# Cutting the last row of a streamed loss kernel into six pieces instead of seven

## The chip, the cores and the metric

One core of a Trainium2 chip runs the kernel. The metric is the device time of one execution in microseconds (us). A time is the median of several runs, with lowest and highest in brackets where they matter.

In the traces the semaphore of each load got 16 updates, spread over 0.38 to 0.44 us in the old kernel's profile. Here a load counts as landed at the last of them, when its semaphore is full. Where a text counts "from the row-6 landing", it means the moment at which the last load before the changed part (row 6 of the target) has landed.

## The reference

```python
batch, dim = 1024, 4096
log_input = randn(batch, dim) as float32
target    = randint(0, 10, (batch, dim)) as float32

def reference(log_input, target):
    loss = np.exp(log_input) - target * log_input
    return np.mean(loss, axis=-1).astype(np.float32)
```

Two arrays of 16 MiB are read once, and 4 KiB are written.

## The kernel before

Each of the 128 partitions owns eight rows of 4096 columns. x is `log_input`, t is `target`. Rows 0 to 6 are loaded in large transfers; the last row (row 7) is cut into pieces, given in units of 32 columns:

```python
TAIL = [("x", 98), ("t", 50), ("t", 48), ("x", 24), ("t", 18), ("x", 6), ("t", 12)]
# ... cut ...
for what, w in TAIL:
    loads.append((what, at[what], w * d // 128))
    at[what] += w * d // 128
```

All loads go out in this order from one queue. ScalarE (ACT in the profile) takes exp of each x piece and sums it along the row; VectorE (DVE) multiplies each t piece with its x and sums -t*x. In the profile each of these is followed by a short row with READ_ACCUMULATOR in its name (0.08 us on DVE, 0.19 on ACT), whose output is one column:

```python
nc.vector.tensor_tensor_reduce(            # every product but the last
    out=place("t", lo, w), in0=place("t", lo, w), in1=place("x", lo, w),
    scale=-1.0, op0=ALU.mult, op1=ALU.add, accum_out=...   # cut
).wait_op(landed[i], 16, "sem-ge").then_inc(
    prod_done if j < n_t - 2 else last_ready, 1)
```

The partial sums of row 7 are written into spare columns right behind the last piece of t, opposite columns of x that hold -1. So one last product over the last t piece and these columns gives the finished mean, and it must wait for three things at once:

```python
nc.vector.tensor_tensor_reduce(            # the last product
    in0=place("t", lo, w + n_parts), in1=place("x", lo, w + n_parts),
    scale=-inv_d, op0=ALU.mult, op1=ALU.add,               # cut
    accum_out=all_loss[:, last_row : last_row + 1],
).wait_op(last_ready, 18, "sem-ge")        # 16: its own load; 1: last exp sum; 1: last product sum
```

Then SP, which issues all 14 transfers in the profile, stores the 4 KiB result.

## Time and profile before

| | before |
|---|---|
| time | 83.93 us (83.86 to 84.18, 3 runs) |
| span in the profile | 82.5 us |
| load queue | 2016 packets, 33.56 MB, 95.8% of 16 engines' span |
| DVE busy / ACT busy | 43% / 40% |

The span is counted from the first load to the last instruction; the time is about 1.34 us longer (83.89 for the profiled run of span 82.545). Busy shares of DVE and ACT are averages over the whole span and say little here: DVE waited 45.4 us of the span for loads and ACT 23.6, and both matter only in the last microseconds (in the 10 us windows from 40 to 80 us the DMA share was 0.98 to 1.01). The prediction below shows the lines themselves.

### The profile page before, as it was taken

The numbers are of one execution on the slowest core, as the hardware profiler recorded it, in microseconds if no ns is written. First come the engines' busy times: TensorE is split into PE (matmuls) and PEld (weight loads), VectorE is DVE, ScalarE is ACT, GpSimd is POOL, SyncE is SP. The second block draws the span as 40 slices with busy tenths as digits, with TensorE's granted clock in tenths as the row PEclk, the third lists the DMA queues.
The fourth block names the chain that finished last, engine by engine and source line by source line (L and its number), as shares of the span: only waits on it lengthen the run. The fifth ranks groups of instructions, "written<-read, shape, count | busy, mean of one in ns | idle before, by whom it ended". The sixth has DMA issues, their size and how long they took to land.

```text
span 82.5 us, 131 instructions
## 1 busy us (share of the span) xinstructions
DVE 35.6 (43%) x22; ACT 33.2 (40%) x35; POOL 0.3 (0%) x5
## 2 busy tenths in 40 slices
DVE  0000000000000000000099999999369995993992
ACT  0500000000499920000000998979792496009460
POOL 0000000000000000000000000000000000000000
DMA  9289999929999992999599799799799999999960
GB/s 508 127 381 508 508 508 508 476 95 445 508 508 508 508 413 95 508 508 508 254 508 429 333 508 492 318 460 508 302 453 397 461 421 418 426 402 412 397 231 2
DMA packets 2016, 33.56 MB, mean 407 GB/s; under 512 B 352, under 2 KB 608, under 8 KB 1120
## 3 DMA queue, kind: packets, MB, share of 16 engines
q1 hardware_dynamic: 2016, 33.56, 95.8%
HBM read 33.55 MB, written 0.00 MB: 407 GB/s over the span
## 4 chain that ended last, share of the span: by engine, by line
DMA 72%; DVE 18%; issue 5%; SPq 3%; DVEq 0%
DMA t_big<-in_target_dram 49%; DMA x_big<-in_log_input_dram 23%; DVE t_big L175 17%; SPq L129 3%; DVE t_big L193 1%; DVE parts L175 0%; DVEq L192 0%; SPq L127 0%; DVE all_loss L193 0%
## 5 line engine op out<-in xcount | busy, mean ns | idle before, releaser
L175 DVE CUSTOM_DVE_ANT_0 t_big<-t_big,x_big 128x4096 f32<-128x4096 f32 (+3 forms) x8 | 26.2, 3308 | 43.5 <-DMA t_big<-in_target_dram 43.4
L155 ACT ACTIVATE e_dump<-x_big 128x4096 f32<-128x4096 f32 (+3 forms) x8 | 21.8, 2729 | 23.9 <-DMA x_big<-in_log_input_dram 23.6
L141 ACT ACTIVATE join_dump<-parts 128x2 f32<-128x2 f32 x7 | 1.4, 203 | 20.4 <-DVE parts L175 20.3
L175 DVE CUSTOM_DVE_ANT_0 t_mid<-t_mid,x_mid 128x4096 f32<-128x4096 f32 x2 | 8.8, 4424 | 2.0 <-DMA t_mid<-in_target_dram 2.0
L155 ACT ACTIVATE e_dump<-x_mid 128x4096 f32<-128x4096 f32 x2 | 7.1, 3568 | 0.0
L155 ACT ACT_TABLE_LOAD x1 | 1.3, 1283 | 2.9 <-PEq L48 2.9
L155 ACT ACTIVATION_READ_ACCUMULATOR e_dump<-x_big 128x1 f32 x8 | 1.5, 186 | 0.0
L141 ACT ACTIVATION_READ_ACCUMULATOR join_dump<-parts 128x1 f32 x7 | 1.3, 186 | 0.0
L175 DVE DVE_READ_ACCUMULATOR2_ANT parts<- 128x1 f32 x7 | 0.6, 84 | 0.0
L193 DVE CUSTOM_DVE_ANT_0 t_big<-t_big,x_big 128x390 f32<-128x390 f32 x1 | 0.6, 566 | 0.0
L155 ACT ACTIVATION_READ_ACCUMULATOR e_dump<-x_mid 128x1 f32 x2 | 0.4, 186 | 0.0
L175 DVE DVE_READ_ACCUMULATOR2_ANT t_big<- 128x1 f32 x3 | 0.2, 82 | 0.0
L136 POOL MEMSET x_big<- 128x6 f32 x1 | 0.1, 104 | 2.5 <-POOLq L48 2.5
L227 POOL MEMSET const-uint8-127<- 128x1 uint8 x1 | 0.1, 102 | 0.0
L227 POOL MEMSET const-bfloat16-1.0<- 128x1 bf16 x1 | 0.1, 101 | 0.0
L227 POOL MEMSET const-float32-0.0<- 128x1 f32 x1 | 0.1, 98 | 0.2 <-issue 0.2
L227 POOL MEMSET const-float32-1.0<- 128x1 f32 x1 | 0.1, 98 | 0.0
L193 DVE DVE_READ_ACCUMULATOR2_ANT all_loss<- 128x1 f32 x1 | 0.1, 82 | 0.0
## 6 DMA issues: line engine op xcount, KB each, us to landing
x_mid<-in_log_input_dram SPq DMA_DIRECT2D x1, 4096.0 KB, 49.9
t_mid<-in_target_dram SPq DMA_DIRECT2D x1, 4096.0 KB, 59.2
x_big<-in_log_input_dram SPq DMA_DIRECT2D x1, 2048.0 KB, 19.8
t_big<-in_target_dram SPq DMA_DIRECT2D x1, 2048.0 KB, 24.3
x_big<-in_log_input_dram SPq DMA_DIRECT2D x1, 1568.0 KB, 15.4
t_big<-in_target_dram SPq DMA_DIRECT2D x1, 800.0 KB, 17.0
t_big<-in_target_dram SPq DMA_DIRECT2D x1, 768.0 KB, 18.4
x_big<-in_log_input_dram SPq DMA_DIRECT2D x1, 384.0 KB, 18.9
```

The costliest lines, as they stand in the source:

```text
L129: dma = nc.sync.dma_start(out=place(what, lo, w), in_=src[:, lo : lo + w])
L136: nc.gpsimd.memset(big["x"][:, 4 * d : 4 * d + n_parts], -1.0).then_inc(ones_done, 1)
L141: nc.scalar.activation(out=join_dump[:, 2 * row : 2 * row + 2], in_=parts[:, 2 * row : 2 * row + 2], func=ACT_F.Copy, scale=inv_d, accum_o ...
L155: nc.scalar.activation(out=e_dump[:, col : col + w], in_=place("x", lo, w), func=ACT_F.Exp, bias=0.0, scale=1.0, accum_out=parts[:, 2 * ro ...
L175: nc.vector.tensor_tensor_reduce(out=place("t", lo, w), in0=place("t", lo, w), in1=place("x", lo, w), scale=-1.0, scalar=0.0, op0=ALU.mult ...
L193: nc.vector.tensor_tensor_reduce(out=place("t", lo, w + n_parts), in0=place("t", lo, w + n_parts), in1=place("x", lo, w + n_parts), scale= ...
L227: nc = _bacc.Bacc("TRN2", target_bir_lowering=False, num_devices=1)
```

## The change

Merging the 192-column x piece into the x pieces before it (128 columns go to the second, 64 to the first) saves one transfer and one exp. The t pieces are made a little larger in front, and the last two equal.

```diff
-TAIL = [("x", 98), ("t", 50), ("t", 48), ("x", 24), ("t", 18), ("x", 6), ("t", 12)]
+TAIL = [("x", 100), ("t", 52), ("t", 48), ("x", 28), ("t", 14), ("t", 14)]
```

In columns: x 3136, t 1600, t 1536, x 768, t 576, x 192, t 384 become x 3200, t 1664, t 1536, x 896, t 448, t 448.

## The prediction

Its sum: +151 (landing) - 133 (second-last product) + 65 (last product) = +83 ns, which takes 83.93 to 84.01 us. Its slopes and fixed costs are fits to the old kernel's profile: 159 ns + 1.0417 ns a column to the DVE products, 175 + 0.833 to the exps, 65 ns a piece + 1.18 a column to the landings. That an engine serves 8 partitions is the division of a piece's 128 packets by the 16 engines of the profile page; it fits the trace, in which eight packets of 16384 bytes (median 611 ns each) make 4888 ns and the row-6 t landed 4891 ns after the row-6 x.

> **What bounds the kernel now.** I read the page's chain of work first, then the queue table, then the timeline of the last 9 us, then the waits, and last the trace's records of when each transfer's semaphore became full.
>
> The chain of the page says that almost three quarters of the span is transfer time:
>
> ```profile
> ## 4 chain that ended last, share of the span: by engine, by line
> DMA 72%; DVE 18%; issue 5%; SPq 3%; DVEq 0%
> ...
> q1 hardware_dynamic: 2016, 33.56, 95.8%
> ```
>
> The reader should see a single queue that keeps its 16 engines busy for 95.8% of the span while it moves 33.56 MB. All work is paced by this stream, and the change moves no byte more or less. So the only time that the cut of the last row can change is what remains between the stream's last pieces and the end. The timeline of that stretch:
>
> ```profile
> 74.10 2.79 ACT L155 ACTIVATE e_dump<-x_big 128x3136 f32<-128x3136 f32 x1 [4.44 <-DMA x_big<-in_log_input_dram]
> ...
> 76.05 1.83 DVE L175 CUSTOM_DVE_ANT_0 t_big<-t_big,x_big 128x1600 f32<-128x1600 f32 x1 [1.28 <-DMA t_big<-in_target_dram]
> ...
> 77.94 1.76 DVE L175 CUSTOM_DVE_ANT_0 t_big<-t_big,x_big 128x1536 f32<-128x1536 f32 x1
> 78.93 0.81 ACT L155 ACTIVATE e_dump<-x_big 128x768 f32<-128x768 f32 x1 [1.53 <-DMA x_big<-in_log_input_dram]
> ...
> 79.70 0.76 DVE L175 CUSTOM_DVE_ANT_0 t_big<-t_big,x_big 128x576 f32<-128x576 f32 x1
> 79.97 0.33 ACT L155 ACTIVATE e_dump<-x_big 128x192 f32<-128x192 f32 x1
> 80.24 0.19 ACT L155 ACTIVATION_READ_ACCUMULATOR e_dump<-x_big 128x1 f32 x1
> 80.38 0.08 DVE L175 DVE_READ_ACCUMULATOR2_ANT t_big<- 128x1 f32 x1
> 80.50 0.57 DVE L193 CUSTOM_DVE_ANT_0 t_big<-t_big,x_big 128x390 f32<-128x390 f32 x1
> ```
>
> The columns are start, duration, engine, line, operation. VectorE (DVE) sums -target*x for each piece of t, ScalarE (ACT) sums exp for each piece of x, and the last DVE instruction (L193) takes the last t piece together with the partial sums in the columns after it. It starts when three things are there: its own t piece, the last exp sum, and the last product sum. The landing records (semaphore full, us from the span's start) give what the timeline rounds off or leaves unnamed:
>
> ```
> t row 6   x3136    t1600    t1536    x768     t576     x192     t384
> 70.306    74.074   76.022   77.915   78.903   79.674   79.950   80.440
> ```
>
> Each of the t1600, t1536 and t576 products starts 23 ns after its own landing (76.045, 77.938, 79.697 in the records), so each is released by the stream and not by DVE. The last one starts at 80.498. Its t384 landed at 80.440 (usable at 80.463), the exp sum of x192 was ready at 80.430, and the product sum of t576 at 80.464, 34 ns before the start. All three end within 34 ns of each other: the old cut is balanced. The chain in order of time shows the same knot:
>
> ```profile
> 80.38 0.09 DVE t_big L175
> 80.47 0.02 issue
> 80.50 0.57 DVE t_big L193
> 81.06 0.01 DVE all_loss L193
> ```
>
> By time, the DVE accumulator read is the last of the three and the t384 landing is right behind it. What sets the end is therefore: landing of the second-last t piece, its product, the hand-over, the last product, the output store.
>
> [...] this is a custom multiply-and-sum: 1826 ns for 1600, 1759 for 1536, 759 for 576, 566 for 390, which is 159 ns + 1.0417 ns a column within 1 ns. [...] The trace has 2788 ns for 3136, 815 for 768, 334 for 192, or 175 + 0.833 a column[...]. [...] x192 lands 276 ns after its predecessor, of which its bytes take about 226. [...] 16 updates per piece, spread over about 0.4 us; I use the last.
>
> **The change part by part.**
>
> 1. The stream. The landing intervals of the pieces (4891 ns for 4096 columns, 3768 for 3136, 276 for 192, and so on) fit 0.0369 ns a byte and engine plus about 65 ns a piece, with misfits up to 29 ns. One column is 4 bytes in each of the 128 partitions, of which an engine serves 8, so 64 columns are 2048 bytes an engine, about 76 ns. Up to and including the second-last t piece there are five pieces before and five after. Columns before: 3136 + 1600 + 1536 + 768 + 576 = 7616; after: 3200 + 1664 + 1536 + 896 + 448 = 7744. That is 128 more, or 151 ns: the second-last t lands at 79.674 + 0.151 = 79.825. The removed x192 stood after that point in the queue, so removing it does not help this piece. The very last landing has the same bytes in front of it and one piece fewer: 80.440 - 0.065 = 80.375.
>
> 2. The second-last product. It starts at 79.825 + 0.023 = 79.848. DVE is free for it: t1664 lands at 76.022 + 0.151 = 76.173 and starts at 76.196; t1536 lands 0.151 later than before, at 78.066, and starts at 78.089. Two rows of 4096 back to back start 4.345 us apart where one lasts 4.42, so DVE accepts the next op some 75 ns before the reported end: at 78.089 + 1.759 - 0.075 = 79.773. The start is still set by the landing, with 75 ns to spare. It lasts 159 + 1.0417 x 448 = 626 ns in place of 759, a saving of 133. It ends at 80.474. The hand-over (end of this product to the start of the last one, 80.456 to 80.498) costs 42 ns as before: 80.516.
>
> 3. The last product. It has 448 columns plus 5 partial sums, 453 in place of 390: 159 + 1.0417 x 453 = 631 ns, 65 more. It ends at 81.147 instead of 81.064.
>
> 4. ScalarE. One exp and one accumulator read go (334 and 186 ns), on an engine with gaps. The 896 exp takes 175 + 0.833 x 896 = 921 ns. x896 lands at 78.903 + 0.302 = 79.205 (64 + 64 + 128 columns more); with 23 ns of start and the read's 0.12 us after the exp ends, its sum is there at about 80.27. Before it was 80.43. ScalarE leaves the knot with 0.2 us in hand, and that gains nothing, since DVE comes later.
>
> 5. Issue and the rest. SP issues one DMA fewer (about 0.45 us), all before 62 us, while the tail first moves at 69.4. The waits that the DVE sequencer makes ahead of the last product end at 80.05 before, and come no later now, since x192's landing is no longer one of them. The store after the end is unchanged.
>
> The sum: +151 (landing) - 133 (second-last product) + 65 (last product) = +83 ns. From the median of 83.93 this makes 84.01 us. The even cut 448/448 only looks better balanced: the last DVE product waits for DVE and is now longer, while the landing in front of it is 0.12 us early.
>
> **The rivals.**
>
> A. The last landing is the bound. Then removing a transfer pays: the last product would start at 80.375 + 0.023 = 80.398 and end at 81.029, 35 ns earlier, 83.90 us. For it: the landing was only 35 ns from being the bound. Against it: DVE works on the second-last piece until 80.47 and is one engine; it could hold only if that piece came over 0.1 us earlier than I work out.
>
> B. Fewer and larger pieces speed up the stream as a whole. The packet times in the trace go from 36 ns for 768 bytes to 470 for 12544, which leaves about 8 ns a packet, some 62 ns for the eight of a piece. So this is the same 65 ns a piece, and it falls behind the second-last t. If half of it still reached that piece, the gain would be 30 ns: 83.98.
>
> C. DVE becomes a chain of its own: if the t1536 landing is more than 75 ns later than I think, the two short products follow it back to back. Each 0.1 us beyond would add 0.1 us: 84.1. For it: the slack of 75 ns is small. Against it: the landings of both move together.
>
> D. The stream's own scatter. The three runs lie between 83.86 and 84.18, so 0.3 us is to be had without any change, more than A, B and C differ by.
>
> **Range and chances.** The estimate is 84.01. The terms from landing intervals carry about 30 ns each, the runs' scatter is about 0.15, so 83.80 to 84.25 should hold it 8 times in 10. 2% is 1.68 us; the whole stretch from the first tail landing that differs to the end is only some 7 us and nearly all of it stays, so I give 0.01 to faster, 0.98 to within 2%, 0.01 to slower.
>
> **What would show it.** Right: the 448 product starts near 79.85 just behind its landing and takes 0.63; the last one starts near 80.52, about 34 ns after the accumulator read of the product before it and over 0.1 us after its landing; it takes 0.63; the exp of 896 ends with its sum by 80.3. Wrong: a last product that starts on its landing (A), landings of the second-last t well before 79.8 (B), or a 448 product that starts later than 23 ns after its landing (C). A fully different transfer rate before 70 us would move all of it, and would be no effect of this change.

## The result, and the profile after

The changed kernel took 84.09 us (83.96 to 84.17, 6 runs), the old one 83.97 (83.86 to 84.18, 6 runs) in the same rounds. The ratio is 1.0008, with a 95% interval of 0.9991 to 1.0024. Ratios here and below are as recorded: they compare the mean times of both kernels' fast runs of the same rounds, so they are not quite the ratio of the medians.

The page of the changed kernel, its queue and its chain of work:

```profile
q1 hardware_dynamic: 1872, 33.56, 95.3%
...
DMA 70%; DVE 22%; issue 5%; SPq 1%; DVEq 0%
```

There are 144 packets fewer (in the traces 128 of data and 16 of 4 bytes), the same 33.56 MB, and the stream is still the bound. The timeline of the last stretch (start, duration, engine, line, operation):

```profile
76.39 1.89 DVE L175 CUSTOM_DVE_ANT_0 t_big<-t_big,x_big 128x1664 f32<-128x1664 f32 x1 [1.45 <-DMA t_big<-in_target_dram]
...
78.28 1.76 DVE L175 CUSTOM_DVE_ANT_0 t_big<-t_big,x_big 128x1536 f32<-128x1536 f32 x1
79.46 0.92 ACT L155 ACTIVATE e_dump<-x_big 128x896 f32<-128x896 f32 x1 [1.75 <-DMA x_big<-in_log_input_dram]
...
80.01 0.63 DVE L175 CUSTOM_DVE_ANT_0 t_big<-t_big,x_big 128x448 f32<-128x448 f32 x1
80.32 0.19 ACT L155 ACTIVATION_READ_ACCUMULATOR e_dump<-x_big 128x1 f32 x1
80.56 0.08 DVE L175 DVE_READ_ACCUMULATOR2_ANT t_big<- 128x1 f32 x1
80.68 0.63 DVE L193 CUSTOM_DVE_ANT_0 t_big<-t_big,x_big 128x453 f32<-128x453 f32 x1
```

The ACT row of 0.19 us now ends at 80.51, well ahead of the last product; the DVE row of 0.08 us is the one that ends right before it. The chain in order of time, at its end:

```profile
59.23 17.14 DMA t_big<-in_target_dram
...
76.39 3.10 DVE t_big L175 x3
...
80.56 0.09 DVE t_big L175
80.65 0.02 issue
80.68 0.63 DVE t_big L193
81.31 0.01 DVE all_loss L193
```

This chain does not name the landing of the second-last t: from the t1664 landing, 76.369 in the records below, it follows DVE's own products. The landing records tell the two apart. The 448 product started at 80.007, 23 ns after its landing at 79.984, and DVE was free for it 41 ns earlier, at 79.966, where the accumulator read of the 1536 product began (in the seven-piece cut below, a product held up by DVE starts together with this read). So the landing is the later of the two, by little.

The landing records (semaphore full, us from the span's start):

```
         t row 6  x3200   t1664   t1536   x896    t448    t448
changed  70.484   74.335  76.369  78.257  79.440  79.984  80.532
```

The span is 0.24 us longer, 82.785 in place of 82.545. Of this, 0.178 is already there at the row-6 landing (70.484 against 70.306), in loads that the change does not touch. Only the rest, 0.062, comes after it: the last product ends 10.823 us after the row-6 landing in place of 10.758, 0.065 later.

### The profile page after: what moved, and what is told of

Read it like the earlier page. It is cut to its first block, busy times and chain, and to the rows that moved or that the text cites. A ratio compares the mean times of both kernels' runs of the same rounds, so it can differ in the third digit from the quotient of the medians.

```text
span 82.8 us, 128 instructions
## 1 busy us (share of the span) xinstructions
DVE 35.6 (43%) x22; ACT 32.9 (40%) x33; POOL 0.3 (0%) x5
## 2 busy tenths in 40 slices
DMA packets 1872, 33.56 MB, mean 405 GB/s; under 512 B 336, under 2 KB 592, under 8 KB 976
## 3 DMA queue, kind: packets, MB, share of 16 engines
q1 hardware_dynamic: 1872, 33.56, 95.3%
## 4 chain that ended last, share of the span: by engine, by line
DMA 70%; DVE 22%; issue 5%; SPq 1%; DVEq 0%
DMA t_big<-in_target_dram 70%; DVE t_big L175 21%; SPq L129 1%; DVE t_big L193 1%; DVE parts L175 0%; DVEq L192 0%; SPq L127 0%; DVE all_loss L193 0%
## 5 line engine op out<-in xcount | busy, mean ns | idle before, releaser
L155 ACT ACTIVATE e_dump<-x_big 128x4096 f32<-128x4096 f32 (+2 forms) x7 | 21.7, 3095 | 24.2 <-DMA x_big<-in_log_input_dram 24.0
L155 ACT ACT_TABLE_LOAD x1 | 1.3, 1283 | 3.0 <-PEq L48 3.0
L193 DVE CUSTOM_DVE_ANT_0 t_big<-t_big,x_big 128x453 f32<-128x453 f32 x1 | 0.6, 631 | 0.0
```

The source lines that it names most:

```text
L155: nc.scalar.activation(out=e_dump[:, col : col + w], in_=place("x", lo, w), func=ACT_F.Exp, bias=0.0, scale=1.0, accum_out=parts[:, 2 * ro ...
L193: nc.vector.tensor_tensor_reduce(out=place("t", lo, w + n_parts), in0=place("t", lo, w + n_parts), in1=place("x", lo, w + n_parts), scale= ...
```

## The experiments

All 12 runs gave correct results. The table puts them beside the profiles of both kernels; all but the last two columns are nanoseconds from the row-6 landing, read from the trace's records.

| kernel (t and x pieces of the tail differ as told below) | second-last t landed | last t landed | last product starts | ends | time, us | ratio to old, 95% interval |
|---|---|---|---|---|---|---|
| old, first profile | 9368 | 10134 | 10192 | 10758 | 83.97 | |
| changed, first profile | 9500 | 10048 | 10192 | 10823 | 84.09 | 1.0008 (0.9991 to 1.0024) |
| changed, again | 9495 | 10038 | 10185 | 10816 | 84.11 | 0.9988 (0.9966 to 1.0010) |
| merge alone | 9593 | 10054 | 10416 | 10982 | 84.26 | 1.0008 (0.9988 to 1.0028) |
| new sizes, seven pieces | 9307 | 10111 | 10142 | 10774 | 84.04 | 0.9984 (0.9964 to 1.0005) |
| last piece smaller | 9676 | 10042 | 10501 | 11000 | 84.37 | 1.0022 (0.9998 to 1.0045) |
| old, again | 9367 | 10136 | 10191 | 10757 | 84.06 | 1.0012 (0.9992 to 1.0032) |
| last load in two | 9498 | 10102 | 10190 | 10822 | 84.16 | 1.0017 (1.0005 to 1.0029) |
| four pieces | 7034 | 10160 | 10192 | 11687 | 84.77 | 1.0086 (1.0071 to 1.0100) |
| eight pieces | 9877 | 10132 | 10269 | 10701 | 83.98 | 0.9992 (0.9980 to 1.0004) |
| last piece larger | 9524 | 10223 | 10247 | 11013 | 84.12 | 1.0004 (0.9983 to 1.0025) |
| four pieces, again | 6815 | 9949 | 9974 | 11470 | 84.68 | 1.0072 (1.0050 to 1.0094) |
| old, third profile | 9418 | 10118 | 10243 | 10808 | one run | |
| eight pieces, again | 9861 | 10137 | 10266 | 10698 | 83.96 | 0.9987 (0.9973 to 1.0000) |

The theory is the prediction's: the path goes through the second-last t landing and then both products one after the other. The main rival is that the last landing sets the end, so that a transfer saved is time saved.

### Control: the changed kernel again

No edit.

> The changed kernel once more, as control. Counting from the landing of the row-6 t load, the old kernel ended its last product at 10.758 us and the changed one at 10.823. Theory (the last product waits for the DVE product before it): again 10.82 within 0.03, last product starting 34 ns after the accumulator read before it and 0.1 us or more after its own landing; ratio to before about 1.0008. Rival (the change of 0.12 us in the medians is only scatter of the early stream): the 0.065 in the tail would not return.

It ended at 10.816, the last product started 34 ns after the sum of the product before it (10.151) and 147 ns after its own landing. So the tail returned as it was. The ratio did not: 0.9988, on the other side of 1. Its runs lie between 83.92 and 84.25 and the old kernel's eleven between 84.04 and 84.65. The whole time does not resolve an effect of 0.08%; the trace from the row-6 landing does much better.

### Control: the old kernel again, twice

No edit.

> The old kernel once more, as control of the method. Theory: the tail repeats to 0.03 us (last product ends 10.76 us after the row-6 landing) whatever the whole time does, and the whole time scatters with the landing of row 6. The ratio to the old kernel's own runs should be 1.000; how far it is off says what a ratio can tell here.

> One more profile of the old kernel, to see where its row-6 t load lands: 70.31 and 70.27 us in its two profiles, 70.44 to 70.59 in eight profiles of altered cuts. Theory (scatter of loads that no cut touches; the old kernel's profiles happened to be of fast runs): anywhere in 70.25 to 70.75, and its tail again 10.76. Rival (the altered kernels really start later): again 70.27 to 70.31.

Measured against its own earlier copy the old kernel has a ratio of 1.0012, with an interval of 0.4% from end to end. This is the floor below which I take no ratio to mean anything. The tail ended at 10.757 and at 10.808 (10.76 was expected both times). The 0.05 of the third profile is one landing: the second-last t at 9.418 in place of 9.368. From that landing to the end the three profiles take 1390, 1390 and 1390 ns. So the engines' part repeats to the nanosecond and the stream's part to about 50. The third profile is from another chip than the second, so that the 50 ns may lie between chips as well as between executions.

The row-6 landing was 70.306, 70.273 and 70.352 in the three profiles of the old kernel, and 70.443 to 70.627 in all altered ones but one. That looks like an effect of the edit, but the altered kernel of four pieces, again, has 70.292. Also, if the old kernel's medians beside the other kernels (83.97, 84.14, 84.01, 84.03 and 84.10) are taken back to the row-6 landing with the fixed distances of the traces (time less 1.34 less about 12.24 from row 6 to the span's end), they stand for 70.39, 70.56, 70.43, 70.45 and 70.52. So the reading is scatter, and that the old kernel's profiles fell on faster runs. It is likely, not proved.

### The merge alone

Shown against the old kernel:

```diff
-TAIL = [("x", 98), ("t", 50), ("t", 48), ("x", 24), ("t", 18), ("x", 6), ("t", 12)]
+TAIL = [("x", 98), ("t", 50), ("t", 48), ("x", 30), ("t", 18), ("t", 12)]
```

> Only the merge: the 192-column x piece joins the 768 one (x 3136, t 1600, t 1536, x 960, t 576, t 384), all t pieces as before. Theory: 192 columns (227 ns of transfer) now stand ahead of the second-last t, whose product is the path, so the last product ends 0.22 us later than in the old kernel (10.98 after the row-6 landing), ratio 1.0027. Rival (the last landing is the bound): it comes 0.065 to 0.085 us earlier, so the end is as much earlier: 10.68, ratio 0.999.

The end came at 10.982, as the theory has it to 2 ns, and the rival's 10.68 is out. Saving a transfer and an exp made the tail 0.22 us longer, because the 192 columns of x moved ahead of the t piece on the path: it landed at 9.593 in place of 9.367 to 9.418. The chain of this run shows that piece as the root, the wait for its product (0.55 us of "issue", 80.20 to 80.75), the sum, and the last product:

```profile
60.64 19.41 DMA t_big<-in_target_dram
...
80.20 0.55 issue
80.75 0.09 DVE t_big L175
80.85 0.02 issue
80.87 0.57 DVE t_big L193
```

Its last t load was there at 80.507 by the landing records, 0.36 us before the product that needs it started. The ratio, 1.0008, is less than the expected 1.0027, which lies just inside its interval.

### The sizes alone, with seven pieces

```diff
-TAIL = [("x", 100), ("t", 52), ("t", 48), ("x", 28), ("t", 14), ("t", 14)]
+TAIL = [("x", 100), ("t", 52), ("t", 48), ("x", 22), ("t", 14), ("x", 6), ("t", 14)]
```

> Only the sizes, still seven pieces (x 3200, t 1664, t 1536, x 704, t 448, x 192, t 448). Theory: second-last t lands 0.23 us earlier than in the changed kernel, so its product becomes bound by DVE itself (about 75 ns after the landing would have allowed) and the last product by its landing: end 10.79 after the row-6 landing, 0.03 earlier than the changed kernel and 0.03 later than the old one. Rival (one piece fewer is what counts): end at least 0.065 later than the changed kernel, 10.89.

The end came at 10.774 (expected 10.79; the rival 10.89). One more transfer and one more exp than in the changed kernel, and the tail is 0.042 to 0.049 us shorter. The second-last product no longer follows its landing:

```profile
80.01 0.08 DVE L175 DVE_READ_ACCUMULATOR2_ANT t_big<- 128x1 f32 x1
80.01 0.62 DVE L175 CUSTOM_DVE_ANT_0 t_big<-t_big,x_big 128x448 f32<-128x448 f32 x1
```

It starts together with the accumulator read of the 1536 product, 0.170 us after its own landing at 79.839: here DVE itself is in the way. The last product then starts at 10.142, with its landing usable at 10.134 (10.111 and the usual 23 ns) and the sum before it done at 10.107, some 35 ns earlier. The two differ by 8 ns in what they would have allowed, so which of them was last is not to be told apart.

### The last two pieces shifted, both ways

```diff
 # last piece smaller
-TAIL = [("x", 100), ("t", 52), ("t", 48), ("x", 28), ("t", 14), ("t", 14)]
+TAIL = [("x", 100), ("t", 52), ("t", 48), ("x", 28), ("t", 18), ("t", 10)]
 # last piece larger
+TAIL = [("x", 100), ("t", 52), ("t", 48), ("x", 28), ("t", 10), ("t", 18)]
```

> The changed kernel with its last two t pieces 576 and 320 in place of 448 and 448. Theory (bound by the second-last landing and both products in a row): that landing is 0.15 us later, the sum of the two products is unchanged, end 10.97 after the row-6 landing, 0.15 later than the changed kernel. Rival (bound by the last landing): that landing doesn't move and the last product is 0.13 us shorter, end 10.69 or earlier.

> The changed kernel with its last two t pieces 320 and 576 in place of 448 and 448, the opposite shift to 576 and 320, which cost 0.18 us in the tail. Theory (the end is the later of two paths: the second-last landing with both products, and the last landing with the last product): the second-last landing comes 0.15 us earlier, so the last product now waits for its own landing, which does not move (10.04 after the row-6 landing), and takes 764 ns; start 10.07, end 10.83, 0.01 later than the changed kernel. Rival (only the path through the second-last landing exists): 0.15 us earlier than the changed kernel, 10.67.

With the smaller last piece the end came at 11.000, 0.18 later than in the changed kernel, although the last landing did not move (10.042) and the last product is 0.13 us shorter. Expected was 10.97; the second-last t landed 0.18 later where 0.15 was expected. The rival's 10.69 is out. The chain's end shows a 0.50 us product that waits for a product of 576 columns:

```profile
60.73 19.47 DMA t_big<-in_target_dram
...
80.91 0.10 DVE t_big L175
81.00 0.02 issue
81.03 0.50 DVE t_big L193
```

With the larger last piece the run was disturbed before the point of interest: its first tail load landed at 4.008 in place of 3.823 to 3.851, and it was the slowest of the kernel's six runs. What follows that landing is as in the others (6.215 to the last landing, against 6.197), so 0.16 has to be taken off: the end at 11.013 becomes 10.85, against 10.83 expected and 10.67 of the rival. The verdict does not need this correction, since it rests on what started the last product:

```profile
80.10 0.49 DVE L175 CUSTOM_DVE_ANT_0 t_big<-t_big,x_big 128x320 f32<-128x320 f32 x1
...
80.51 0.08 DVE L175 DVE_READ_ACCUMULATOR2_ANT t_big<- 128x1 f32 x1
80.70 0.77 DVE L193 CUSTOM_DVE_ANT_0 t_big<-t_big,x_big 128x581 f32<-128x581 f32 x1
```

The product sum was ready at 10.142 and the exp sum at 10.142, but the last product started at 10.247, which is 24 ns after its landing at 10.223. Here the last landing is the bound. So both paths exist, and in the changed kernel they are 0.12 us apart.

### The last load in two transfers

```diff
+        if i == len(loads) - 1:
+            for a in (lo, lo + w // 2):        # two transfers of 224 columns
+                dma = nc.sync.dma_start(out=place(what, a, w // 2), in_=src[:, a : a + w // 2])
+                dma.then_inc(last_ready, 16)
+            continue
 # ... cut ...
-            ).wait_op(last_ready, 18, "sem-ge").then_inc(loss_done, 1)
+            ).wait_op(last_ready, 34, "sem-ge").then_inc(loss_done, 1)
```

> The changed kernel with its last t load of 448 columns sent as two transfers of 224, still one product. It adds one transfer's fixed cost at the very end and nothing to either product. Theory (the last product waits for the product before it, with about 0.12 us to spare over its landing): last landing 0.06 later (10.11 after the row-6 landing), end unchanged at 10.82. Rival (the last landing is the bound): end 0.06 later, 10.88.

The last landing moved by 54 to 64 ns (10.102 against 10.048 and 10.038), which is what the one transfer more cost, and the end stayed: 10.822 against 10.823 and 10.816. That is the slack of the last landing shown directly. The last product still follows the accumulator read:

```profile
80.61 0.08 DVE L182 DVE_READ_ACCUMULATOR2_ANT t_big<- 128x1 f32 x1
80.72 0.63 DVE L200 CUSTOM_DVE_ANT_0 t_big<-t_big,x_big 128x453 f32<-128x453 f32 x1
```

The time, 84.16, is above the old kernel's 84.01 with an interval of 1.0005 to 1.0029. The tail's 0.05 to 0.065 (0.06% to 0.08%) lies inside it, but the old kernel came out at 1.0012 against itself in the same rounds, so this ratio is no proof of it.

### A coarse cut of four pieces, twice

```diff
+TAIL = [("x", 88), ("t", 88), ("x", 40), ("t", 40)]
```

> A coarse cut of four pieces (x 2816, t 2816, x 1280, t 1280), to see what the cut is worth where it is far from the knot. Theory: the last landing is only about 0.2 us earlier than in the old kernel (three pieces fewer, 9.92 after the row-6 landing), while the last product has 1282 columns and waits for a product of 2816; end about 11.47, 0.7 later than the old kernel, ratio 1.0085. Rival (pieces cost, fewer are better): end earlier than the old kernel.

> The coarse cut once more, since its profiled run had a first tail landing 0.24 us later than its bytes explain and was the slowest of its four. Theory (a disturbance of that run alone): landings at about 3.39, 6.79, 8.36 and 9.92 us after the row-6 landing, last product starting 34 ns after the product before it, end 11.45. Rival (loads of 2816 columns are slow in themselves): first landing again at 3.63, end 11.69.

The first run's profile was of a disturbed execution (85.11 us, the others 84.69 to 84.79), with single packets of up to 635 ns where the median of that size was 422. The second has the landings at 3.427, 6.815, 8.387 and 9.949, up to 0.04 later than expected, and the end at 11.470, as expected to 0.02. Three pieces fewer brought the last landing forward by 169 to 187 ns, that is 56 to 62 ns a piece. It did not help, for the last product now has 1283 columns:

```profile
80.15 0.08 DVE L175 DVE_READ_ACCUMULATOR2_ANT t_big<- 128x1 f32 x1
80.27 1.50 DVE L193 CUSTOM_DVE_ANT_0 t_big<-t_big,x_big 128x1283 f32<-128x1283 f32 x1
```

The ratios are 1.0086 and 1.0072, clear of noise.

### A cut of eight pieces, twice

Since pieces are cheap (about 60 ns of stream each) and a column in the last product costs 1.04 ns, the same sum was used to look for a better cut.

```diff
+TAIL = [("x", 97), ("t", 51), ("t", 46), ("x", 21), ("t", 18), ("x", 10), ("t", 5), ("t", 8)]
```

> A cut found with the sum of the prediction (65 ns a piece, 1.18 ns of transfer a column, both products' 159 ns + 1.0417 a column): x 3104, t 1632, t 1472, x 672, t 576, x 320, t 160, t 256, eight pieces. Theory: last landing 0.06 later than in the old kernel but a last product of only 262 columns; end 0.055 earlier than the old kernel, 10.70 after the row-6 landing, ratio 0.9993, which is below what the times resolve. Rival (one more piece costs): end 0.06 or more later than the old kernel.

> The cut of eight pieces once more, since it ended its tail 0.057 us earlier than the old kernel's first profile, while the old kernel's three profiles scatter by 0.05 through one landing. Theory: end at 10.70 within 0.03, of which the stretch from the second-last t landing (9.88) to the end repeats to 5 ns (0.824); median some 0.05 below that of the old kernel's runs beside it, ratio 0.9994, not resolved. Rival (the first profile was a lucky one): end at 10.76 or later.

The tail ended at 10.701 and 10.698, which is 0.06 to 0.11 earlier than the old kernel's (10.757 to 10.808) and 0.12 earlier than the changed one's. Expected was 10.70. The last rows of the first of the two:

```profile
80.34 0.33 DVE L175 CUSTOM_DVE_ANT_0 t_big<-t_big,x_big 128x160 f32<-128x160 f32 x1
80.47 0.19 ACT L155 ACTIVATION_READ_ACCUMULATOR e_dump<-x_big 128x1 f32 x1
80.59 0.08 DVE L175 DVE_READ_ACCUMULATOR2_ANT t_big<- 128x1 f32 x1
80.71 0.43 DVE L193 CUSTOM_DVE_ANT_0 t_big<-t_big,x_big 128x263 f32<-128x263 f32 x1
```

One detail was missed: the stretch from the second-last t landing was to repeat to 5 ns and took 0.824 and 0.837. In the second run this landing came 16 ns earlier, but DVE was held by the product before, so its product began no sooner. The times are 83.98 against 84.01 and 83.96 against 84.10; the ratios 0.9992 and 0.9987 have intervals that reach 1.0004 and 1.0000. So by its tail this version is ahead of both kernels, and by its times it is not shown to be: about 0.1 us is what a time of 84 us hides.

## Why the prediction was right

The prediction was 84.01 us, 0.08 above the old kernel, within 2%. The median came out at 84.09, and at 84.11 in later rounds. That the first comparison (1.0008) agrees with +0.08 us is luck: the second gave 0.9988, which is 0.1 us the other way. What can be tested is the sum of the tail. By its steps, with times from the row-6 landing so that the two profiles can be compared:

1. The stream up to the second-last t was to carry 128 columns more and no piece fewer: 151 ns. Measured: 9.368 to 9.500, 132 ns, and against the other profiles of the old kernel 77 to 133 (9.418 to 9.367, against 9.495 and 9.500). The direction is shown by the merge alone, which put 192 columns ahead of this piece and moved it by 175 to 226 ns against the three old profiles, where 227 were expected. The size of this term is what the stream's scatter makes uncertain.
2. The second-last product was to be 133 ns shorter and to start 23 ns after its landing. It took 626 in place of 759 ns and started at 9.523, 23 ns after 9.500. The 75 ns for which DVE was to be free before came out smaller: the 1536 product started at 7.797, and 1.759 - 0.075 later is 9.481, so 42 ns. This did not matter, as it stayed positive.
3. The hand-over was 43 ns (42 predicted), and the last product 631 ns (631 predicted).
4. ScalarE's sum was ready at 10.022, 0.17 ahead of the last product, and gained nothing. It was predicted for about 80.27 on the old kernel's clock, 9.96 from the row-6 landing; x896 landed 0.06 later than worked out. The prediction's sign "by 80.3" was thus missed by 0.03 in this profile and met in the second (9.983, or 80.29), without any effect on the end.
5. The last landing came 86 ns earlier (65 predicted), and the last product started 0.12 after it could have used it, as predicted.

The sum was to be +83 ns in the tail and was +65 in the first pair of profiles; the mean of the old kernel's three is 10.774 and of the changed one's two 10.820, which makes +45. Of the terms, the engines' part is exact: from the second-last t landing to the end 1390 ns before and 1323 and 1321 after, 67 to 69 less, where -133 and +65 make 68. All of the miss lies in the landing term, 132 in place of 151 in the first pair.

The rivals: A (the last landing is the bound) fell with the merge alone, the smaller last piece and the load in two. It is right for another cut, the larger last piece, 128 columns away. B (the saved transfer speeds up the piece on the path) fell with the load in two: one transfer more behind that piece left its landing at 9.498, against 9.500 and 9.495. The merge alone, where the piece came later by its bytes, agrees, but its scatter of 50 ns would hide B's 30. C (DVE becomes a chain of its own) did not happen in the changed kernel, with some 40 ns to spare, and did in the seven-piece cut of the same sizes. D, the scatter, is what the whole times show most of: the two comparisons of old and changed kernel gave 1.0008 and 0.9988. All three tails with the changed order of pieces (10.816, 10.822 and 10.823, the load in two among them) end later than all three of the old kernel (10.757, 10.758 and 10.808), the nearest pair by 8 ns. So as far as six profiles can show it the change makes the tail longer, by 0.01 to 0.07 us; that it makes the whole kernel slower is not resolved by the times.

## What to carry to other kernels

Where a stream is the bound, list for its last pieces when each lands and what must still happen after it, and take the latest of these sums. Here a transfer saved behind the piece on that path gained nothing, and columns moved ahead of it cost their bytes. The last landing moved by 54 to 64 ns for one queued transfer more (the load in two), by 56 to 62 for each of three fewer (the four pieces), and by 64 to 98 for the one fewer of the change and of the merge alone. The ends of the altered tails were reckoned to 30 ns from a slope and a fixed cost per engine, the disturbed profiles aside. To test so small an effect, compare traces from a landing shortly before the change: the tails repeated to 50 ns where whole times of one kernel scattered by 300 to 600.
